# The feed-forward projection scaled in place in its PSUM bank, and the causal convolution reading it from there

## The chip, the cores and the metric

The kernel runs on one core of one Trainium2 chip. The metric is the device time of one execution in microseconds, as the median of several runs. The profile that goes with it records one execution on that core: every instruction of TensorE (PE, with its weight loads as PEld), VectorE (DVE), ScalarE (ACT), GpSimd (POOL) and SyncE (SP, which issues transfers), with its start, its length and the line of the kernel that it comes from.

## The reference

A decoder trunk of two layers over 512 positions of 1024 features, in float32. Layer 0 mixes with a dilated sliding-window attention, layer 1 with a state-space scan; each mixer is followed by a gated feed-forward layer with a short causal convolution, and the trunk ends in an RMS norm. What the change touches is the feed-forward layer:

```python
def rmsnorm(x, w):
    y = x * lax.rsqrt(jnp.mean(x * x, axis=-1, keepdims=True) + NORM_EPS)
    return y * w

def causal_depthwise_conv(x, w, b):        # w: (3, channels) here
    k = w.shape[0]
    y = lax.conv_general_dilated(x, w[:, None, :], window_strides=(1,), padding=[(k - 1, 0)],
        dimension_numbers=("NWC", "WIO", "NWC"), feature_group_count=x.shape[-1])
    return y + b

def conv_ffn(h, w_up, conv_w, conv_b, w_down):
    u = causal_depthwise_conv(h @ w_up, conv_w, conv_b)
    gate, up = u[..., :D_FF], u[..., D_FF:]
    return (jax.nn.silu(gate) * up) @ w_down
```

with h = rmsnorm(x, ffn_norm_w), 2 x 2816 projected channels, and x = x + conv_ffn(h).

## The kernel before

Everything is kept transposed: features on the 128 partitions, the 512 positions along the free axis. The residual x is eight tiles xr (128 x 512). Every large product is made as three matmuls of float32r parts (`mm3`, line 136): the weights and the operand are each split into a high and a low part, and high x high, high x low and low x high are added up in one bank. So one *unit* of a projection, that is 128 output channels for all positions, takes 8 x 3 = 24 matmuls into one bank of 512 float32 columns (`project`, 146).

The norm is applied late. The operand of the projection is x times the norm's weight, split into xh and xl (`split`, 212); the factor 1/rms of each position is worked out while the projection already runs (`inv_rms`, 228), transposed along the free axis on TensorE (`along_free`, 256) and copied to the tile rbc by ScalarE (line 185 for layer 0, line 1046 for layer 1). Each finished unit is then multiplied by rbc.

PSUM has three rings of banks: "mm" with three banks (`mm_bank`, 67), "aux" with three, "side" with two. Units and down projections take turns in the mm ring. At the start of a feed-forward layer the first units cannot be scaled until rbc is there. In layer 0 `norm_and_project` (158) puts unit 0 into an mm bank and units 1 and 2 into side banks; in layer 1 `last_rows` (993) does the same for units 0, 1 and 2 and puts unit 3 into an mm bank, with four of its eight steps ahead of the transposition of the norm's factor and four behind it.

A feed-forward layer (`ffn`, 610) has 44 units, gate and up by turns, in three parts of 16, 16 and 12 units. For each unit:

- `load_unit` (116): SyncE's queue brings 512 KB of weights (line 121), ScalarE casts them to the high part hi (125), VectorE subtracts to get the low part lo (126).
- TensorE: 24 matmuls into the unit's bank p (134).
- VectorE, line 620: us = p x rbc, from the bank into an SBUF tile us, a ring of three tiles.
- `conv` (602) reads us: ScalarE makes the tile a from the last tap's weight and the bias (603), then VectorE adds the two shifted taps, first over 511 columns, then over 510 (605).

For each pair ScalarE applies silu to the gate (624), GpSimd multiplies it with the up half (627), ScalarE and GpSimd split the product into high and low parts (629, 630). After each part, `down` (263) makes the eight output tiles from those parts with two output tiles open at a time, and VectorE adds them to xr (640). The third part of layer 1 goes into the last norm and the output (`finish`, 1059).

The order of the instructions is not written out, except where a manual_schedule block fixes an engine's own order: TensorE's in `norm_and_project`, `last_rows` and the down projections. Elsewhere a scheduler orders each engine's list at build time by a simulated timeline, with the rings of tiles and banks as it goes; what it chose is what the trace shows. Each engine then works through its list in order, and waits for the instruction at its head.

Of the kernel before, what the change touches and what calls it, by code (L numbers as in the profile page):

```python
# [12 lines left out]
ALU = mybir.AluOpType  # L13
# [27 lines left out]
C_FCW = C_SCB + 32  # L41
C_FCB = C_FCW + 2 * 44 * 3
# [9 lines left out]
def trunk(ctx: ExitStack, tc: tile.TileContext, A, out):  # L52
    nc = tc.nc
    V, SC, G, T = nc.vector, nc.scalar, nc.gpsimd, nc.tensor
# [21 lines left out]
    def t2(name, tag, bufs, pool=k2, dtype=F32):  # L76
        return pool.tile([P, 512], dtype, tag=tag, name=name, bufs=bufs)
# [3 lines left out]
    def high_low(name):  # L81

        high = t2(f"{name}h", "high", 8, dtype=F32R)
        if not kept:
            k2.tile([P, 32], F32, tag="gap3", name="gap3", bufs=1)
        kept.append(name)
        return high, t2(f"{name}l", "low", 8, dtype=F32R)
# [13 lines left out]
    rbc = cp.tile([P, S], F32, tag="rbc", name="rbc")  # L101
# [8 lines left out]
    def col(c):  # L110
        return par[:, c : c + 1]
# [4 lines left out]
    def load_unit(src, name, n=1024, pieces=1, low=V, at=0):  # L116
        raw = wr.tile([P, 1024], F32, tag="raw", name=f"raw_{name}")
        hi, lo = (wh.tile([P, 1088], F32R, tag=t, name=f"{t}_{name}")[:, at : at + 1024] for t in ("hi", "lo"))
        for i in range(pieces):
            s = slice(i * n // pieces, (i + 1) * n // pieces)  # L120
            dma(raw[:, s], src[:, s])
            if i < pieces - 1:
                V.tensor_copy(hi[:, s], raw[:, s])
            else:
                SC.copy(hi[:, s], raw[:, s])  # L125
            low.tensor_tensor(lo[:, s], raw[:, s], hi.bitcast(F32)[:, s], op=ALU.subtract)  # L126
        return hi, lo
# [18 lines left out]
    def project(src, name, low=V, cut=None):  # L146

        if name in early:
            return early.pop(name)
        hi, lo = loaded.pop(name) if name in loaded else load_unit(src, name, low=low)  # L150
        t = mm_bank(name)
        for k in range(KD):
            if cut and cut[0] == k:
                cut[1]()
            mm3(t, hi, lo, k, xh[k], xl[k], k == 0, k == KD - 1)
        return t
# [106 lines left out]
    def down(n, load, ms, operand, kn, done, width=512, depth=1, late=False):  # L263

        held = []

        def finish():
            m, p, hi, lo, at = held.pop(0)
            mm3(p, hi, lo, at + kn - 1, *operand(kn - 1), kn == 1, True)
            done(m, p)  # L270

        for m in ms:
            hi, lo, at = load(m)
            p = mm_bank(f"{n}{m}")[:, :width]
            for c in range(kn - 1):
                if late and m == 2 and c == 3:
                    finish()
                    finish()
                mm3(p, hi, lo, at + c, *operand(c), c == 0, False)
            if len(held) == depth and not (late and m == 1):  # L280
                finish()
            held.append((m, p, hi, lo, at))
        while held:
            finish()
# [302 lines left out]
    lp = ctx.enter_context(tc.tile_pool(name="lp", bufs=1, reuse_waits="tile"))  # L587
# [5 lines left out]
    for m in range(KD):  # L593
        if m not in wo_held:
            wo_first(m)
        hi, lo, p = wo_held[m]
# [5 lines left out]
    def conv(dst, src, c_w, c_b, taps):  # L602
        SC.activation(dst, src, AF.Identity, bias=col(c_b), scale=col(c_w + taps - 1))  # L603
        for j in range(1, taps):
            V.scalar_tensor_tensor(  # L605
                dst[:, j:], src[:, : S - j], col(c_w + taps - 1 - j), dst[:, j:],
                op0=ALU.mult, op1=ALU.add,
            )

    def ffn(layer, done):  # L610
        for part, (c0, cn) in enumerate(FF_PARTS):
            gh, gl = [], []
            for c in range(c0, c0 + cn):
                ab = []
                for gu in range(2):
                    i = 2 * c + gu
                    n = f"u{layer}_{i}"
                    p = project(A["wup"][layer * 44 + i], n)
                    us = t2("us" + n, "us", 3, lp)
                    V.tensor_tensor(us, p, rbc, op=ALU.mult)  # L620
                    a = t2("a" + n, "a", 13, lp)
                    conv(a, us, C_FCW + (layer * 44 + i) * 3, C_FCB + layer * 44 + i, 3)
                    ab.append(a)
                SC.activation(ab[0], ab[0], AF.Silu)

                by = V if layer == 1 and c == NFF - 1 else G
                by.tensor_tensor(ab[1], ab[0], ab[1], op=ALU.mult)  # L627
                g_h, g_l = high_low(f"g{c}")
                SC.copy(g_h, ab[1])
                by.tensor_tensor(g_l, ab[1], g_h.bitcast(F32), op=ALU.subtract)  # L630
                gh.append(g_h)
                gl.append(g_l)
            n = cn * P

            def load(m):
                i = (layer * len(FF_PARTS) + part) * KD + m
                return (*load_unit(A["wdn"][i][:, :n], f"wd{i}", n), 0)

            def add(m, p):
                V.tensor_tensor(xr[m], xr[m], p, op=ALU.add)  # L640
                if part == len(FF_PARTS) - 1:
                    done(m)

            if layer == 1 and part == len(FF_PARTS) - 1:
                finish(load, lambda c: (gh[c], gl[c]), cn)
                return
            with tc.manual_schedule(engines={mybir.EngineType.PE}):
                down(f"wd{layer}{part}", load, range(KD), lambda c: (gh[c], gl[c]), cn, add, late=True)
# [4 lines left out]
    norm_and_project(ssum, ups(0, range(3)), ups(0, (3, 4)))  # L653
    ssum_a = t2("ssum2", "ssum", 2)
    ffn(0, lambda m: prep(m, xr[m], C_MIX + KD, ssum_a))
    norm_and_project(ssum_a, [(A["win"][0], "xs00"), (A["wdt"], "wdt"), (A["win"][2], "b0")], [(A["win"][3], "c0"), (A["win"][1], "xs01")])

# [401 lines left out]
    def finish(load, operand, cn):  # L1059
# [72 lines left out]
        for b in range(2):  # L1132
            for j in range(2):
# [6 lines left out]
                queue.dma_start(out[1][j, :, b * 512 : (b + 1) * 512], o)  # L1140

    ffn(1, None)


# [101 lines left out]
```

## Time and profile before

| | |
|---|---|
| median of 3 runs | 1626.72 us (1626.13 to 1626.76) |
| the profiled execution | 1626.55 us |
| its span, first to last instruction | 1624.6 us |
| TensorE busy | 1615.7 us, 99% of the span |
| VectorE busy | 1082.8 us, 67% |
| ScalarE busy | 655.0 us, 40% |
| GpSimd busy | 418.6 us, 26% |
| mean granted TensorE clock | 0.999 |

Busy time of TensorE counts the whole length of a matmul, and matmuls overlap: one lasts 0.38 us by the profile, and the next starts 0.22 us after it. A row of the chain or of a timeline gives the start in us from the span's first instruction, the length in us and what ran; "x3" is three instructions in a row, and what stands in brackets is the idle time of the engine before it with what ended it. The names are those of the kernel's tiles with their numbers left out: u is a unit's bank, usu its us tile, au its a tile, hi_u and lo_u its weights.

### The profile page before, as it was taken

The numbers are of one execution on the slowest core, as the hardware profiler recorded it, in microseconds if no ns is written. First come the engines' busy times: TensorE is split into PE (matmuls) and PEld (weight loads), VectorE is DVE, ScalarE is ACT, GpSimd is POOL, SyncE is SP. The second block draws the span as 40 slices with busy tenths as digits, with TensorE's granted clock in tenths as the row PEclk, the third lists the DMA queues.
The fourth block names the chain that finished last, engine by engine and source line by source line (L and its number), as shares of the span: only waits on it lengthen the run. The fifth ranks groups of instructions, "written<-read, shape, count | busy, mean of one in ns | idle before, by whom it ended". The sixth has DMA issues, their size and how long they took to land.

```text
span 1624.6 us, 21067 instructions
## 1 busy us (share of the span) xinstructions
PE 1615.7 (99%) x8038; PEld 1382.9 (85%) x8038; DVE 1082.8 (67%) x1813; ACT 655.0 (40%) x965; POOL 418.6 (26%) x272
## 2 busy tenths in 40 slices
PE   9999999999999999999999999999999999999998
PEld 8888888888888888888887888888888888888887
DVE  6366665266647855764657899988897784574564
ACT  5233332333334532432445455544443442342343
POOL 0444453045402320220231222222111341121020
PEclk9999999999999999999999999999999999999999
DMA  7322222222224323223233433334332232332321
GB/s 259 98 80 83 78 91 80 96 85 79 78 78 134 113 91 105 103 81 117 81 101 104 148 108 115 100 100 127 114 126 90 93 104 91 104 104 91 104 78 52
DMA packets 53235, 165.13 MB, mean 102 GB/s; under 512 B 6224, under 2 KB 9680, under 8 KB 53136
## 3 DMA queue, kind: packets, MB, share of 16 engines
q1 hardware_dynamic: 52304, 163.01, 30.5%
q8 instruction: 63, 1.03, 0.3%
q10 hardware_dynamic: 832, 0.79, 0.1%
q14 instruction: 36, 0.29, 0.1%
HBM read 161.62 MB, written 2.16 MB: 101 GB/s over the span
## 4 chain that ended last, share of the span: by engine, by line
PE 99%; ACT 0%; DVE 0%; POOL 0%; POOLq 0%; DVEq 0%; issue 0%
PE u L134 29%; PE qk L134 16%; PE wd L134 12%; PE v L134 8%; PE xs L134 5%; PE z L134 5%; PE wso L134 5%; PE wo L134 3%; PE c L134 3%; PE b L134 3%; PE wz L134 2%; PE py L830 1%; PE pg L490 1%; PE pp L477 1%; PE po L485 1%; PE pf L838 1%
## 5 line engine op out<-in xcount | busy, mean ns | idle before, releaser
L134 PE MATMUL u<-xh,lo_u 128*128 128x512 f32 x704 | 268.9, 382 | 0.0
L134 PE MATMUL u<-xh,hi_u 128*128 128x512 f32 x704 | 268.8, 382 | 0.0
L134 PE MATMUL u<-xl,hi_u 128*128 128x512 f32 x704 | 266.3, 378 | 0.0
L627 POOL TENSOR_TENSOR au<-au,au 128x512 f32<-128x512 f32 x43 | 58.5, 1360 | 422.2 <-DVE au L605 396.6
L605 DVE SCALAR_TENSOR_TENSOR au<-usu,par,au 128x511 f32<-128x511 f32 (+1 forms) x176 | 159.4, 911 | 7.6 <-ACT au L603 2.9
L125 ACT CAST hi_u<-raw_u 128x1024 fp32r<-128x1024 f32 x88 | 91.1, 1044 | 168.4 <-PE u L134 95.6
L388 POOL TENSOR_TENSOR rotqk<-rotqk,sr 32x512 f32<-32x512 f32 x48 | 88.2, 1837 | 250.2 <-DVE rotqk L387 239.8
L134 PEld LDWEIGHTS u<-xl,hi_u 128*128 128x128 f32 x704 | 131.7, 187 | 24.5
L134 PEld LDWEIGHTS u<-xh,lo_u 128*128 128x128 f32 x704 | 131.7, 187 | 24.0
L134 PEld LDWEIGHTS u<-xh,hi_u 128*128 128x128 f32 x704 | 131.7, 187 | 21.8 <-issue 0.4
L134 PE MATMUL qk<-xh,hi_qk 128*128 128x512 f32 x384 | 148.6, 387 | 0.0
L134 PE MATMUL qk<-xh,lo_qk 128*128 128x512 f32 x384 | 147.1, 383 | 0.0
L134 PE MATMUL qk<-xl,hi_qk 128*128 128x512 f32 x384 | 145.6, 379 | 0.0
L126 DVE TENSOR_TENSOR lo_u<-raw_u,hi_u 128x1024 fp32r<-128x1024 f32 x88 | 113.8, 1299 | 29.9 <-ACT hi_u L125 29.9
L620 DVE TENSOR_TENSOR usu<-u,rbc 128x512 f32<-128x512 f32 x88 | 60.3, 690 | 93.1 <-PE u L134 86.4
L640 DVE TENSOR_TENSOR xr<-xr,wd 128x512 f32<-128x512 f32 x40 | 27.3, 688 | 116.9 <-PE wd L134 116.9
L125 ACT CAST hi_qk<-raw_qk 128x1024 fp32r<-128x1024 f32 x48 | 50.3, 1047 | 130.3 <-PE qk L134 69.3
L134 PEld LDWEIGHTS qk<-xh,lo_qk 128*128 128x128 f32 x384 | 71.8, 187 | 13.3
L134 PEld LDWEIGHTS qk<-xl,hi_qk 128*128 128x128 f32 x384 | 71.9, 187 | 12.8
L389 POOL TENSOR_TENSOR qk<-qk,rotqk 32x512 f32<-32x512 f32 x48 | 81.5, 1698 | 3.8
L125 ACT CAST hi_wd<-raw_wd 128x1024 fp32r<-128x1024 f32 (+1 forms) x48 | 46.1, 972 | 88.7 <-PE wd L134 55.6
L134 PEld LDWEIGHTS qk<-xh,hi_qk 128*128 128x128 f32 x384 | 71.9, 187 | 11.2
(647 smaller groups left out, 3768.5 us busy)
## 6 DMA issues: line engine op xcount, KB each, us to landing
raw_u<-in_wup SPq DMA_DIRECT2D x88, 512.0 KB, 3.3
raw_qk<-in_wqk SPq DMA_DIRECT2D x48, 512.0 KB, 3.3
raw_wd<-in_wdn SPq DMA_DIRECT2D x32, 512.0 KB, 3.2
raw_xs<-in_win SPq DMA_DIRECT2D x16, 512.0 KB, 3.3
raw_z<-in_win SPq DMA_DIRECT2D x16, 512.0 KB, 3.4
lm<-rows SPq DMA_DIRECT2D x32, 256.0 KB, 5.4
raw_wso<-in_wso SPq DMA_DIRECT2D x16, 512.0 KB, 3.3
raw_v<-in_wv SPq DMA_DIRECT2D x12, 512.0 KB, 3.5
```

Of the source, the lines that this page charges most:

```text
L125: SC.copy(hi[:, s], raw[:, s])
L126: low.tensor_tensor(lo[:, s], raw[:, s], hi.bitcast(F32)[:, s], op=ALU.subtract)
L134: T.matmul(in_turns(dst), w, in_turns(x), start=first, stop=last)
L388: G.tensor_tensor(rot[R, :], rot[R, :], sr[R, :], op=ALU.mult)
L389: G.tensor_tensor(at(t)[R], at(t)[R], of(rot)[R], op=ALU.add)
L477: T.transpose(pp[:, b * P : (b + 1) * P], pr[:, b * P : (b + 1) * P], ident)
L485: T.matmul(po[:, ii], v0[h][:, b * P : (b + 1) * P], pts[i][:, (b - i + 1) * P : (b - i + 2) * P], start=b == max(i - 1, 0), stop=b == i,)
L490: T.matmul(pg[:, ii], vt[g, half][i][:, es], pts[i][:, (g + 1) * P : (g + 2) * P], start=g == 1, stop=g == 2,)
L605: V.scalar_tensor_tensor(dst[:, j:], src[:, : S - j], col(c_w + taps - 1 - j), dst[:, j:], op0=ALU.mult, op1=ALU.add,)
L620: V.tensor_tensor(us, p, rbc, op=ALU.mult)
L627: by.tensor_tensor(ab[1], ab[0], ab[1], op=ALU.mult)
L640: V.tensor_tensor(xr[m], xr[m], p, op=ALU.add)
```

## The change

In the feed-forward layers the product with rbc is written back into the unit's bank, and `conv` is given the bank in place of the us tile. The us ring stays for the state-space layer, which uses it at other lines. Nothing else is edited.

```diff
                     i = 2 * c + gu
                     n = f"u{layer}_{i}"
                     p = project(A["wup"][layer * 44 + i], n)
-                    us = t2("us" + n, "us", 3, lp)
-                    V.tensor_tensor(us, p, rbc, op=ALU.mult)
+                    V.tensor_tensor(p, p, rbc, op=ALU.mult)
                     a = t2("a" + n, "a", 13, lp)
-                    conv(a, us, C_FCW + (layer * 44 + i) * 3, C_FCB + layer * 44 + i, 3)
+                    conv(a, p, C_FCW + (layer * 44 + i) * 3, C_FCB + layer * 44 + i, 3)
                     ab.append(a)
```

Before, the last reader of a unit's bank is line 620. After, the last readers are the activation of line 603 and the two taps of line 605.

## The prediction

> **What bounds the kernel now.** I read the page first, then the chain of work that ended last, then who waited for whom on TensorE. From the page:
>
> ```profile
> span 1624.6 us, 21067 instructions
> PE 1615.7 (99%) x8038; PEld 1382.9 (85%) x8038; DVE 1082.8 (67%) x1813; ACT 655.0 (40%) x965; POOL 418.6 (26%) x272
> ```
>
> The program ends when TensorE has got through its list; 8.9 us of the span are not matmul time. The profiled execution took 1626.55 us, 1.95 more than its span and 0.17 below the median of the three runs, 1626.72. The chain (start, length, what) says how dense the feed-forward layers are:
>
> ```profile
> 513.81 8.45 PE u L134 x38
> ...
> 630.60 84.48 PE u L134 x384
> ...
> 1280.40 8.01 PE u L134 x36
> ...
> 1288.85 61.13 PE u L134 x276
> ```
>
> 384 matmuls in 84.48 us is 0.220 us each, so a unit of 24 (one 128-row slice of the projection, one bank) takes 5.28 us. From 630.60 on nothing interrupts TensorE for 16 units, so nothing can be gained there. The waits on TensorE (in total, times, longest) are four rows, of which the first and the last:
>
> ```profile
> PE warm L327 <- DVE mhalf L107: 1.1, 1, 1.1
> ...
> PE pw L1125 <- DVE ms L252: 0.4, 1, 0.4
> ```
>
> None of them has u in it. The feed-forward projection never visibly waits for its scaling or its convolution; the question is only whether the change makes it wait.
>
> **The change, part by part.** The groups of instructions, by shape (busy us, mean ns, idle before):
>
> ```profile
> L605 DVE SCALAR_TENSOR_TENSOR au<-usu,par,au 128x511 f32<-128x511 f32 x88 | 92.4, 1052 | 4.9 <-ACT au L603 2.9
> L603 ACT ACTIVATE au<-usu,par 128x512 f32<-128x512 f32 x88 | 71.2, 813 | 1.9 <-DVE usu L620 1.4
> L605 DVE SCALAR_TENSOR_TENSOR au<-usu,par,au 128x510 f32<-128x510 f32 x88 | 67.7, 771 | 2.7
> L620 DVE TENSOR_TENSOR usu<-u,rbc 128x512 f32<-128x512 f32 x88 | 60.3, 690 | 93.1 <-PE u L134 86.4 <-ACT rbc L185 6.7
> L225 ACT ACTIVATE sq<-xr 128x512 f32<-128x512 f32 x26 | 16.1, 618 | 6.6 <-DVE xr L1068 6.6
> L849 DVE SCALAR_TENSOR_TENSOR yt<-axs,par,py 128x512 f32<-128x512 f32 x16 | 11.4, 742 | 0.5 <-PE py L830 0.3
> ```
>
> No instruction is added or removed: 88 scalings, 88 activations, 176 taps stay.
>
> *The scaling writes its bank.* No row has VectorE writing a bank. The nearest is L620 itself, 690 ns from a bank into an SBUF tile; I take 690. Below it I allow the 0.58 us of ScalarE's copy from a bank (L1046, below), above it the 1052 ns of the first tap.
>
> *The activation reads the bank.* 813 ns today; ScalarE's 512 columns took 618 ns from SBUF and 0.58 us from a bank, so 0.78 to 0.81, and I take 0.81.
>
> *The taps read the bank.* L849 has one operand in a bank and took 742 ns, no more than the fastest from SBUF; I take 0.74. The mean of 1052 is well above that, so VectorE stands to lose up to 88 x (1052 + 771 - 2 x 742) ns = 29.8 us of busy time. It is worth nothing to the end here, as TensorE waits for none of it; it is cover for the rest. The Trainium skill, "SBUF — State Buffer", section "Who interferes with whom", says a VectorE instruction with at most one SBUF input, outside the two-port modes, does not contend with GpSimd, while one with two does; by it the whole 29.8 us goes, and the sum is as it stands.
>
> *The bank is held longer; this is the cost.* Before, a bank is free again after its scaling. Now it is free after scaling, activation and both taps. The ring has three banks, so a unit's bank is wanted back 2 x 5.28 = 10.56 us after the unit's last matmul. In the run of units the chain needs 0.69 + 0.81 + 2 x 0.74 = 3.0 us of its own and one or two other VectorE instructions between: some 5 us. That is hidden by two units of matmuls, and costs nothing while that cover lasts; the same holds where the down projections take over the ring.
>
> It is not covered where a layer starts. There the units run ahead of the norm: the scale row rbc is not known until four or five units are done, and all chains start at once. Layer 1, VectorE, ScalarE and TensorE:
>
> ```profile
> 1289.31 1.23 DVE L126 TENSOR_TENSOR lo_u<-raw_u,hi_u 128x1024 fp32r<-128x1024 f32 x1 [5.60 <-ACT hi_u L125]
> 1290.45 1.88 DVE L620 TENSOR_TENSOR usu<-u,rbc 128x512 f32<-128x512 f32 x3
> 1292.24 0.74 DVE L605 SCALAR_TENSOR_TENSOR au<-usu,par,au 128x511 f32<-128x511 f32 x1
> 1292.96 1.23 DVE L126 TENSOR_TENSOR lo_u<-raw_u,hi_u 128x1024 fp32r<-128x1024 f32 x1
> 1294.10 2.07 DVE L605 SCALAR_TENSOR_TENSOR au<-usu,par,au 128x510 f32<-128x510 f32 x3
> 1296.09 0.68 DVE L620 TENSOR_TENSOR usu<-u,rbc 128x512 f32<-128x512 f32 x1
> ```
>
> ```profile
> 1289.18 0.58 ACT L1046 COPY rbc<-rb 128x512 f32<-128x512 f32 x1
> 1291.17 0.81 ACT L603 ACTIVATE au<-usu,par 128x512 f32<-128x512 f32 x1 [1.41 <-DVE usu L620]
> 1291.89 1.04 ACT L125 CAST hi_u<-raw_u 128x1024 fp32r<-128x1024 f32 x1
> 1292.83 1.51 ACT L603 ACTIVATE au<-usu,par 128x512 f32<-128x512 f32 x2
> ```
>
> ```profile
> 1291.35 0.39 PE L134 MATMUL u<-xh,hi_u 128*128 128x512 f32 x1
> ...
> 1296.53 0.38 PE L134 MATMUL u<-xh,lo_u 128*128 128x512 f32 x1
> 1296.92 0.46 PE L134 MATMUL u<-xh,hi_u 128*128 128x512 f32 x1
> ```
>
> Units 0, 3 and 4 hold the three banks (1 and 2 lie in side banks). The 36 matmuls between the two small groups of the norm are 12 of unit 3 and all of unit 4; 12 more of unit 3 follow, so 1291.35 is the first matmul of unit 5, which needs bank 0. Its scaling had ended at 1290.45 + 0.68 = 1291.13, just in time. 1296.92 is unit 6, 0.17 us late: unit 3's scaling ended at 1296.77, held up by the ring of three us tiles. That small wait goes with the change; the one in its place is larger.
>
> When does unit 0's second tap end? That hangs on the order the scheduler gives VectorE, and layer 0 shows how it chooses:
>
> ```profile
> 523.35 1.89 DVE L620 TENSOR_TENSOR usu<-u,rbc 128x512 f32<-128x512 f32 x3 [6.71 <-ACT rbc L185]
> 525.15 1.21 DVE L126 TENSOR_TENSOR lo_u<-raw_u,hi_u 128x1024 fp32r<-128x1024 f32 x1
> 526.28 0.74 DVE L605 SCALAR_TENSOR_TENSOR au<-usu,par,au 128x511 f32<-128x511 f32 x1
> 526.95 1.21 DVE L126 TENSOR_TENSOR lo_u<-raw_u,hi_u 128x1024 fp32r<-128x1024 f32 x1
> 528.08 2.72 DVE L605 SCALAR_TENSOR_TENSOR au<-usu,par,au 128x511 f32<-128x511 f32 x4
> ```
>
> ```profile
> 523.21 1.05 ACT L125 CAST hi_u<-raw_u 128x1024 fp32r<-128x1024 f32 x1
> 524.16 0.81 ACT L603 ACTIVATE au<-usu,par 128x512 f32<-128x512 f32 x1
> ...
> 525.81 1.53 ACT L603 ACTIVATE au<-usu,par 128x512 f32<-128x512 f32 x2
> ```
>
> ```profile
> 530.12 0.38 PE L134 MATMUL u<-xh,hi_u 128*128 128x512 f32 x1
> ```
>
> At 525.15 it takes a weight subtraction whose cast ended at 524.26, ahead of unit 0's first tap, ready at 524.97. At 528.08 it takes a first tap (511 columns, unit 1's, ready at about 526.6) ahead of unit 0's second (ready at 527.02). So what has been ready longest goes first, wherever it stands in the code. I carry that over. Steps, start to start: scaling 0.60 (1.79 for three), tap 0.66, weight subtraction 1.14; a freed bank reaches TensorE 0.15 us later (1296.77 to 1296.92).
>
> Layer 1: the us ring no longer limits the scalings, so units 4 (ready before rbc) and 3 (its last matmul is the one before 1291.35, so ready at 1291.5) go ahead of the first tap, ready at 1291.98. 1292.24 + 2 x 0.60 = 1293.44; unit 0's first tap to 1294.10; the weight subtraction, ready at 1292.93, to 1295.24; unit 1's first tap, ready at 1293.64, to 1295.90; unit 0's second ends at 1295.90 + 0.74 = 1296.64. Unit 5 starts at 1296.79 in place of 1291.35, unit 6 at 1296.79 + 5.28 = 1302.07 in place of 1296.92: **+5.15 us**. Unit 3's last tap is seven taps on, 1296.56 + 7 x 0.66 + 0.08 = 1301.3, no further wait. Unit 5's matmul stands at the head of TensorE's list, so all that follows moves with it, and nothing later gives it back: the chain is matmuls to the end.
>
> Layer 0: 525.15 + 1.13 + 0.60 (unit 3's scaling, ready at 524.9, a unit's 5.28 before 530.12) + 0.67 + 1.13 + 2 x 0.66, then 0.74 and 0.15: 530.89, where unit 5 starts at 530.12 today: **+0.8 us**. It is smaller because of the 38 matmuls ahead of the scale row 21 are unit 2's and only 17 unit 3's, so the bank is wanted later.
>
> Sum: 1626.55 + 5.15 + 0.8 = **1632.5 us**. Two lesser things I put at nothing: the us tiles are first used later, so the a tiles move in SBUF, and the state-space layer's matmuls are not fed differently; the transfers on SyncE's queue wait for weight subtractions, which move by no more than TensorE does.
>
> **The rivals.** *The clock falls as well.* TensorE would stand still for 5.3 us. Stretches with TensorE's busy time and the granted clock (after the busy columns):
>
> ```profile
> 865.00:870.00 5.00, 4.28 (x26) 3.43 (x25) 2.53 (x4) 2.72 (x4) 0.62 (x1) 1.00 0.60 197
> 1617.28:1620.69 3.41, 0.98 (x8) 0.75 (x7) 1.78 (x4) 1.27 (x2) 1.13 (x2) 1.00 1.03 342
> 1620.70:1624.60 3.90, 0.00 (x0) 0.00 (x0) 0.00 (x0) 0.00 (x0) 0.00 (x0) 0.50 0.64 236
> ```
>
> 0.7 us of idleness cost no clock; a stretch of 3.41 us with 0.98 busy was followed by half the clock. A stop of 5.3 us has such a stretch in it wherever it is cut. If half pace then lasts one such stretch, 3.41 / 2 = 1.7 us are lost: 1634.2. The Trainium skill, "TensorE: Matmul & The Clock Gate", section "A second HAM failure mode: psum-queue depth-cycling", reports a kernel whose cycling through banks made TensorE idle often enough for the gate to swing; by that rule this case would come out, and the tail's rows agree as far as they go. Against it: it is one stop per layer, not a cycle, and no row has one of this length followed by work.
>
> *The taps go first.* If VectorE runs unit 0's taps as soon as it can, the second ends at 1292.24 + 0.66 + 0.74 = 1293.64, or at 1294.84 with a weight subtraction between, as in the rows; unit 6 starts at 1299.07 to 1300.27, up to 0.5 later if unit 3 is late: +2.2 to +3.9. With layer 0 at 0 to 0.8, 1628.7 to 1631.2, middle 1629.9. For it: the longer chain may weigh with the scheduler once TensorE hangs on it. Against it: layer 0's order.
>
> *Not slower.* The scheduler sees the new wait and does unit 0 first of all: scaling at 1289.76, when rbc is there, then 0.68 + 0.81 + 0.66 + 0.74 + 0.15 = 1292.80, 1.45 late, less the 0.17 that goes: 1627.9, inside 0.2%, with layer 0 at nothing. It decides wherever unit 0's bank comes back before about 1294.7 and layer 0 is hidden. Against it: today a weight subtraction precedes the scaling at 1289.31.
>
> *Faster* could only come from the 0.17 and the few waits elsewhere, which the change does not touch.
>
> **How the numbers follow.** A difference of 0.2%, 3.25 us, is about what a measurement can tell. Forecast as summed: 0.36. With the clock: 0.22. Taps first: 0.24. Not slower: 0.12. Faster 0.03, worse than all (a scaling into a bank at the tap's 1052 ns, five of them ahead, or stops in the run of units) 0.03. Of the taps-first case a third lies under 3.25 us, so same is 0.12 + 0.08 = 0.20, slower 0.77. The range leaves out 0.18: from 1628.6, the bottom of taps first, to 1635.2, the clock's 1634.2 and 1.0 for slower scalings.
>
> **What would show it.** Right: about 5 us between unit 4's or 3's last matmul and unit 5's first, at some 1292 to 1297 of layer 1, with L620 five times in a row before the first tap; a wait of u on VectorE's L605; 0 to 1 us in layer 0; 0.220 us a matmul elsewhere; taps near 742 ns. A clock below 1.00 there decides for that rival. Wrong: no wait on L605 in TensorE's list, or waits all along the run of units.

## The result, and the profile after

The kernel with the change takes 1634.83 us (median of 4 runs, 1633.8 to 1636.88) against 1626.74 for the kernel before beside it (4 runs, 1626.13 to 1626.93): a ratio of 1.0052, with an interval of 1.0035 to 1.0069, so 8.1 us or 0.5% slower. The same kernel, run once more later, gave 1.0048 (1.0036 to 1.0061). The profiled execution took 1633.8 us. Its page:

```profile
span 1632.0 us, 21084 instructions
PE 1617.3 (99%) x8038; PEld 1383.7 (85%) x8038; DVE 1052.1 (64%) x1813; ACT 655.0 (40%) x965; POOL 417.7 (26%) x272
```

VectorE has 30.7 us less to do, the matmuls are as many as before, and the span is 7.4 us longer. Who waited for whom on TensorE (total, times, longest) has one row more than before; the other four are the old ones:

```profile
PE u L134 <- DVE au L605: 5.9, 2, 5.3
...
```

Two waits, then, both on a second tap. TensorE's timeline shows where (start, length, what, and in brackets the idle time before it):

```profile
529.28 0.38 PE L134 MATMUL u<-xh,lo_u 128*128 128x512 f32 x1
530.26 0.46 PE L134 MATMUL u<-xh,hi_u 128*128 128x512 f32 x1 [0.59 <-DVE au L605]
...
1291.22 0.38 PE L134 MATMUL u<-xh,lo_u 128*128 128x512 f32 x1
1296.87 0.77 PE L134 MATMUL u<-xh,hi_u 128*128 128x512 f32 x1 [5.27 <-DVE au L605]
```

Each pair is the last matmul before unit 5 and the first of unit 5. In layer 0 the starts are 0.97 us apart, in layer 1 5.65; at a matmul every 0.22 us that is 0.75 and 5.43 us lost. VectorE's timeline in layer 1, the counterpart of the rows that the order was read from:

```profile
1289.40 1.23 DVE L126 TENSOR_TENSOR lo_u<-raw_u,hi_u 128x1024 fp32r<-128x1024 f32 x1 [5.60 <-ACT hi_u L125]
1290.54 3.08 DVE L619 TENSOR_TENSOR u<-u,rbc 128x512 f32<-128x512 f32 x5
1293.54 0.74 DVE L605 SCALAR_TENSOR_TENSOR au<-u,par,au 128x511 f32<-128x511 f32 x1
1294.19 1.22 DVE L126 TENSOR_TENSOR lo_u<-raw_u,hi_u 128x1024 fp32r<-128x1024 f32 x1
1295.33 6.00 DVE L605 SCALAR_TENSOR_TENSOR au<-u,par,au 128x511 f32<-128x511 f32 x9
```

Five scalings in a row, one tap, a weight subtraction, then taps. The chain of waits leaves TensorE here, runs over exactly these instructions, and comes back with unit 5:

```profile
1290.63 1.49 DVE u L619 x3
1292.12 0.23 issue
1292.34 1.29 DVE u L619 x2
1293.63 0.65 DVE au L605
1294.28 1.13 DVE lo_u L126
1295.41 1.33 DVE au L605 x2
1296.74 0.14 issue
1296.87 60.48 PE u L134 x264
```

The last row holds a second loss. 264 matmuls at 0.22 us are 58.1 us, not 60.48. Cutting the time around the stop into stretches of 3.41 us shows it (start and end; busy us of TensorE and its weight loads, VectorE, ScalarE, GpSimd; then the granted clock, the DMA share and GB/s):

```profile
1291.10:1294.51 3.41, 0.51 (x3) 0.10 (x1) 3.41 (x7) 3.24 (x5) 0.00 (x0) 1.00 0.45 154
1294.51:1297.92 3.41, 1.05 (x3) 0.88 (x4) 3.41 (x5) 1.79 (x3) 0.00 (x0) 0.50 0.43 141
1297.92:1301.33 3.41, 3.41 (x10) 2.64 (x9) 3.41 (x6) 1.15 (x2) 1.78 (x2) 0.50 0.03 13
1301.33:1304.74 3.41, 3.41 (x17) 2.91 (x16) 0.14 (x1) 1.71 (x4) 3.28 (x3) 1.00 0.02 5
```

One stretch nearly without a matmul at full clock, two at half, then full again. Of the two stretches that are filled with matmuls, the one at half clock is touched by 10 of them, the last one by 17. From unit 5's first matmul at 1296.87 to the first one back at 0.22 us, at 1301.54, there are 11 steps in 4.67 us instead of 2.42: 2.25 us lost.

Together: 0.75 + 5.43 + 2.25 - 0.37 = 8.06 us, against 8.1 measured. The 0.37 is what the kernel before lost at this place and the changed one does not: from its first matmul of unit 5, at 1291.35, to its third of unit 6, at 1297.44, it has 26 steps in 6.09 us instead of 5.72. The old wait of 0.17 us at unit 6 is part of it.

A second way to count agrees. From a layer's first projection matmul to the first of its down projection, the traces have 85.56 us before and 86.40 after in layer 0, 89.82 (1260.16 to 1349.98) and 97.11 (1260.25 to 1357.36) in layer 1: +0.84 and +7.29, 8.13 us in all. The rows of the chain for layer 1, two of the kernel before and two of the changed one:

```profile
1260.16 0.66 PE u L134 x3
...
1349.98 15.18 PE wd L134 x69
...
1260.25 0.66 PE u L134 x3
...
1357.36 7.70 PE wd L134 x35
```

This second measure, called the layer's stretch below, is used for the experiments. The spans of the two profiled executions differ by less, 7.4 us. Most of the missing 0.7 us lies ahead of the feed-forward layers, in a part that the change does not touch: this execution of the changed kernel reached the first projection matmul of layer 0 at 502.19 us, the one of the kernel before at 502.80.

The groups by shape answer to the four that were priced (busy us, mean ns, idle before):

```profile
L603 ACT ACTIVATE au<-u,par 128x512 f32<-128x512 f32 x88 | 67.8, 777 | 2.3 <-DVE u L619 1.4
L605 DVE SCALAR_TENSOR_TENSOR au<-u,par,au 128x510 f32<-128x510 f32 x88 | 65.6, 748 | 2.8
L605 DVE SCALAR_TENSOR_TENSOR au<-u,par,au 128x511 f32<-128x511 f32 x88 | 65.4, 746 | 3.9 <-ACT au L603 2.8
L619 DVE TENSOR_TENSOR u<-u,rbc 128x512 f32<-128x512 f32 x88 | 60.9, 698 | 138.8 <-PE u L134 132.1 <-ACT rbc L185 6.7
```

### The profile page after: what moved, and what is told of

Same layout as the page of the kernel before. It is cut to its first block, busy times and chain, and to the rows that moved or that the text cites. A ratio compares the mean times of both kernels' runs of the same rounds, so it can differ in the third digit from the quotient of the medians.

```text
span 1632.0 us, 21084 instructions
## 1 busy us (share of the span) xinstructions
PE 1617.3 (99%) x8038; PEld 1383.7 (85%) x8038; DVE 1052.1 (64%) x1813; ACT 655.0 (40%) x965; POOL 417.7 (26%) x272
## 4 chain that ended last, share of the span: by engine, by line
PE 98%; DVE 1%; ACT 0%; POOL 0%; issue 0%; POOLq 0%; DVEq 0%
PE u L134 28%; PE qk L134 16%; PE wd L134 12%; PE v L134 8%; PE xs L134 5%; PE z L134 5%; PE wso L134 5%; PE wo L134 3%; PE c L134 3%; PE b L134 3%; PE wz L134 2%; PE py L829 1%; PE pg L490 1%; PE pp L477 1%; PE po L485 1%; PE pf L837 1%
## 5 line engine op out<-in xcount | busy, mean ns | idle before, releaser
L619 DVE TENSOR_TENSOR u<-u,rbc 128x512 f32<-128x512 f32 x88 | 60.9, 698 | 138.8 <-PE u L134 132.1
L605 DVE SCALAR_TENSOR_TENSOR au<-u,par,au 128x510 f32<-128x510 f32 (+1 forms) x176 | 130.4, 747 | 6.7 <-ACT au L603 2.8
L126 DVE TENSOR_TENSOR lo_u<-raw_u,hi_u 128x1024 fp32r<-128x1024 f32 x88 | 110.0, 1255 | 27.3 <-ACT hi_u L125 27.3
```

What stands on the lines that cost most here:

```text
L605: V.scalar_tensor_tensor(dst[:, j:], src[:, : S - j], col(c_w + taps - 1 - j), dst[:, j:], op0=ALU.mult, op1=ALU.add,)
L619: V.tensor_tensor(p, p, rbc, op=ALU.mult)
```

## The experiments

**One layer at a time.** Two kernels do the change in one layer only. In the other the us tile stays:

```diff
-                    us = t2("us" + n, "us", 3, lp)
+                    us = p if layer == 0 else t2("us" + n, "us", 3, lp)
```

(`layer == 1` in the second.) Layer 0 alone:

> In place in layer 0 alone; layer 1 keeps its us tiles. If the cost is the stop where a layer starts (0.97 us between two matmuls in layer 0 of the changed kernel, 0.22 in a run, so 0.75 lost): 1627.5 us, with that one stop left and a clock of 1.00 throughout. If the cost comes with every unit that is scaled in place, half of the 8.1 us goes with half of the units: about 1630.8 us.

1627.57 against 1626.31 us, a ratio of 1.0006 (0.9997 to 1.0016). The profiled execution of this run took 5987 us, with the matmuls of a unit at 1.09 to 1.10 us on average, for a reason that its trace does not show. So the kernel was run once more for its trace:

> In place in layer 0 alone, once more for its trace: one stop of 0.97 us at unit 5 of layer 0, no wait of u in layer 1 over 0.3 us, clock 1.00; some 0.8 us over the kernel before.

It took 1627.62 us beside 1626.6, in a single run. TensorE's timeline has the one small stop, layer 0's stretch is 0.93 us longer than in the kernel before, and layer 1's is 89.82 us as there:

```profile
530.02 0.38 PE L134 MATMUL u<-xh,lo_u 128*128 128x512 f32 x1
530.99 0.46 PE L134 MATMUL u<-xh,hi_u 128*128 128x512 f32 x1 [0.59 <-DVE au L605]
```

Layer 1 alone:

> In place in layer 1 alone. Stop at the start of the layer: 5.65 - 0.22 = 5.43 us, plus the slow matmuls behind it (eleven, 2.4 us more than at 0.22 each), less the 0.17 us wait that goes: 1634.4 us, 1632.7 if the clock does not fall in every run. Cost with every unit: about 1630.8 us.

1633.6 against 1626.31, 1.0043 (1.003 to 1.0057): 7.3 us, with a layer 1 stretch of 97.01 (+7.19). By the times, layer 0's part is not clear of noise, as its interval takes in 1. By the stretches the two parts, 0.93 and 7.19, add up to the whole, and layer 1 carries nearly all of it.

**The run of units alone.** In place only from unit 5 of each layer on, which is 78 of the 88 units:

```diff
-                    us = t2("us" + n, "us", 3, lp)
+                    us = p if i >= 5 else t2("us" + n, "us", 3, lp)
```

> Units 0 to 4 of each layer keep their us tiles, all later ones are scaled in place (78 of 88). Stop at the start of the layers: the first banks come back after the scaling as before, so 1626.5 to 1626.9 us, no wait of u on VectorE over 0.3 us, taps from unit 5 on near 742 ns, and VectorE's busy time some 25 us lower than before with nothing gained. Cost with every unit: 78/88 of the 8.1 us, about 1634 us.

1626.37 against 1626.31, 1.0001 (0.9992 to 1.001). TensorE waits four times, as before, and never on a tap. The page shows that most of VectorE's saving is there:

```profile
PE 1616.3 (99%) x8038; PEld 1383.2 (85%) x8038; DVE 1056.3 (65%) x1813; ACT 655.0 (40%) x965; POOL 417.9 (26%) x272
```

So holding the bank longer costs nothing along the run, and 26.5 us less work for VectorE (1082.8 to 1056.3) brings nothing.

**Other banks at the start.** If the cost is that the first units keep their banks too long, taking one of them out of the ring of three must remove it. The auxiliary ring has only the norms' small rows at that time; unit 0 of layer 0 and unit 3 of layer 1 are put there:

```diff
-(side_bank if i else mm_bank)(name)
+(side_bank if i else aux_bank if name[0] == "u" else mm_bank)(name)
...
-side_bank(name) if i in (1, 2) else mm_bank(name)
+side_bank(name) if i in (1, 2) else (aux_bank if i == 3 else mm_bank)(name)
```

> The changed kernel, but with one more bank at each layer's start: unit 0 of layer 0 and unit 3 of layer 1 lie in a bank of the aux ring in place of the mm ring. Unit 5 of each layer then has a free bank. Layer 0: unit 6 wants unit 3's bank at 535.4, free by about 534.3; layer 1: unit 6 wants unit 0's at about 1296.8, free at about 1296.8. So if the cost is the number of banks at the start, both stops go, down to 0.3 us, the clock stays at 1.00, and the time is 1626.5 to 1627.2 us. If the order on VectorE or the in-place writes cost by themselves: over 1630 us.

A miss: 1628.03 against 1626.27, 1.0012 (1.0003 to 1.0021). Both stops are gone, but a new one stands at unit 7 of layer 1, which wants unit 4's bank:

```profile
1301.36 0.38 PE L134 MATMUL u<-xh,lo_u 128*128 128x512 f32 x1
1303.59 0.46 PE L134 MATMUL u<-xh,hi_u 128*128 128x512 f32 x1 [1.85 <-DVE au L605]
```

VectorE's heap of work at the start is not smaller; with TensorE no longer standing still for unit 0, it met the next bank. The 2.23 us between the starts left the clock alone (stretches, columns as above):

```profile
1301.70:1303.59 1.89, 0.04 (x1) 0.03 (x1) 1.89 (x4) 0.95 (x2) 0.66 (x1) 1.00 0.24 50
1303.60:1308.00 4.40, 4.40 (x20) 3.77 (x21) 4.29 (x6) 1.87 (x3) 3.67 (x3) 1.00 0.53 170
```

The next kernel puts unit 4 of layer 1 into that ring too, by one more line in `project`:

```diff
-        t = mm_bank(name)
+        t = (aux_bank if name == "u1_4" else mm_bank)(name)
```

> As the run with one more bank per layer, but in layer 1 unit 4 lies in the aux ring too. There unit 7 still stood 2.0 us for unit 4's bank; now it gets unit 0's, free since about 1296.7, and unit 8 unit 5's, wanted at about 1307 and free at about 1306. If the banks at the start are the whole cost: no wait of u on VectorE over 0.3 us, clock 1.00, within 0.5 us of the kernel before (0.9997 to 1.0003 of it). If in-place units cost anything else, or the backlog only moves on to unit 8: 1 to 2 us over it.

1626.67 against 1626.6, 0.9999 (0.999 to 1.0007). Of the waits one of 0.2 us is left, at unit 8:

```profile
PE u L134 <- DVE au L605: 0.2, 1, 0.2
```

All 88 units are scaled in place here. So the banks of the first units are the whole cost of the change, and with them spared it is, within that interval, neither slower nor faster than before.

**The clock by itself.** To keep TensorE busy in layer 1's stop without touching the wait, 22 matmuls that nobody reads go into an auxiliary bank, written in `last_rows` behind the last matmuls of unit 3:

```diff
         part(3, *range(4, KD))
+        idle = aux_bank("idle")
+        for _ in range(22):
+            long_product(idle, xh[0][:, 0:P], xh[0], True, True)
```

> The changed kernel with 22 matmuls that nobody reads, at TensorE's place behind unit 3 of layer 1, that is in the stop: extra work of 22 x 0.22 = 4.84 us. If the stop is a wait for unit 0's bank and the slow clock comes from the idleness: the fillers vanish in the stop, some 0.6 us of it is left, the clock stays at 1.00, and 2.4 us are won: 1632.7 us. If the clock falls for another reason: 1634.8 us with a slow stretch as before. If TensorE were not really free in the stop: 1634.8 + 4.8 = 1639.6 us.

1633.01 against 1626.31, 1.0042 (1.0026 to 1.0057). By the times alone that cannot be told from the changed kernel. The trace can. The stretches under the fill and after it:

```profile
1291.60:1297.00 5.40, 5.40 (x26) 4.45 (x24) 5.40 (x9) 4.41 (x6) 0.00 (x0) 1.00 0.27 97
1297.70:1301.00 3.30, 3.30 (x15) 2.75 (x16) 3.30 (x6) 0.65 (x2) 0.74 (x1) 1.00 0.35 137
```

The clock stays at 1.00, 15 matmuls are counted in 3.3 us, and layer 1's stretch is 95.02 us, 2.09 less than 97.11. What is left of the loss there, 95.02 - 89.82 = 5.2 us, is the wait alone.

**The order on VectorE.** The prediction rested on scalings of units 3 and 4 going ahead of unit 0's taps. The scheduler can be told to put an instruction behind another; here those two scalings of layer 1 go behind unit 0's last tap (`behind_first` is an ordering edge to it, and nothing for other units):

```diff
+                    with behind_first(layer, (3, 4), i):
-                    V.tensor_tensor(p, p, rbc, op=ALU.mult)
+                        V.tensor_tensor(p, p, rbc, op=ALU.mult)
```

> The changed kernel with only the scalings of units 3 and 4 of layer 1 queued behind unit 0's last tap; the weight subtractions stay free. If those two scalings are what put unit 0's tap late: it ends at about 1294.85 in place of 1296.73, unit 5 starts 1.9 us earlier after a stop of some 3.8 us, and unit 6 waits 0.3 to 1.5 us more for unit 3's bank: 1631 to 1632 us without a fall of the clock, 1633 to 1634 with one. If the backlog only moves on, as in the two runs with a hand-made order: a stop of 5 us or more at unit 6 or 7, and 1635 us or over.

1632.36 against 1626.6, 1.0034 (1.0021 to 1.0048). VectorE's timeline, from unit 0's first tap on:

```profile
1292.50 0.74 DVE L611 SCALAR_TENSOR_TENSOR au<-u,par,au 128x511 f32<-128x511 f32 x1
1293.17 1.23 DVE L126 TENSOR_TENSOR lo_u<-raw_u,hi_u 128x1024 fp32r<-128x1024 f32 x1
1294.31 0.74 DVE L611 SCALAR_TENSOR_TENSOR au<-u,par,au 128x510 f32<-128x510 f32 x1
1294.97 1.29 DVE L627 TENSOR_TENSOR u<-u,rbc 128x512 f32<-128x512 f32 x2
```

Unit 0's second tap ends at 1295.05 instead of about 1296.7, and unit 5 starts at 1295.20. The stop is 3.83 us between starts, and the granted clock differs as well:

```profile
1291.95:1295.36 3.41, 0.16 (x1) 0.19 (x2) 3.41 (x6) 2.75 (x5) 0.00 (x0) 1.00 0.39 142
1295.36:1298.78 3.42, 3.42 (x9) 2.65 (x9) 3.42 (x6) 1.85 (x3) 0.00 (x0) 0.50 0.43 153
1298.78:1302.19 3.41, 3.41 (x17) 2.90 (x16) 2.73 (x5) 1.73 (x3) 2.45 (x2) 1.00 0.02 5
```

One stretch at half clock, not two, and it begins 0.16 us after TensorE is back at work. From 1295.20 to 1298.92 there are 9 steps in 3.72 us instead of 1.98, 1.74 us lost. Layer 1's stretch is 94.79, 2.32 below the changed kernel's: 1.82 of the stop and 0.51 of the clock. The time lies below the 1633 to 1634 us expected with a fall of the clock, as the further wait that was expected at unit 6 did not come.

Two stronger orders were tried before that. In the first, the weight subtractions of units 6 and 7 are put behind unit 0's last tap as well:

```diff
+                    with behind_first(layer, (6, 7), i):
-                    p = project(A["wup"][layer * 44 + i], n)
+                        p = project(A["wup"][layer * 44 + i], n)
```

> The changed kernel with VectorE's order altered in layer 1 alone: the scalings of units 3 and 4 and the weight subtractions of units 6 and 7 queue behind unit 0's last tap. If the length of the stop comes from what ran ahead of that tap: unit 0's last tap ends at about 1293.1 in place of 1296.7, unit 5 starts 3.6 us earlier, and unit 6 waits for unit 3's bank until about 1301.3: two stops of some 2.0 and 2.7 us in place of one of 5.65. The sum is then only 0.8 us shorter, but neither stop is long enough for the clock: 1631.6 us. If the clock falls also after a stop of 2.7 us: about 1633.5. If the order does not matter: 1634.8.

A miss: 1637.09 against 1626.27, 1.0065 (1.0049 to 1.008). Unit 5 now waits only 1.06 us between starts, but unit 6, which wants unit 3's bank, 6.98. On VectorE, the rows after unit 0's taps:

```profile
1293.06 0.69 DVE L628 TENSOR_TENSOR u<-u,rbc 128x512 f32<-128x512 f32 x1
1293.66 3.49 DVE L126 TENSOR_TENSOR lo_u<-raw_u,hi_u 128x1024 fp32r<-128x1024 f32 x3
1297.06 0.70 DVE L628 TENSOR_TENSOR u<-u,rbc 128x512 f32<-128x512 f32 x1
```

By the rule of what has been ready longest, the subtractions that had been put off were then first, and three went ahead of the taps of the next bank. In the second, units 0 and 3 are written first, and the scalings of 1, 2 and 4 and the subtractions of 6 and 7 go behind unit 3's last tap:

```diff
+        if layer == 1:
+            ahead_of.update({i: taps(layer, i) for i in (0, 3)})
...
+        with behind_first(layer, (6, 7), i):
+            p = project(A["wup"][layer * 44 + i], n)
+        with behind_first(layer, (1, 2, 4), i):
+            V.tensor_tensor(p, p, rbc, op=ALU.mult)
```

> As the run before, but units 0 and 3 of layer 1 are both done first (they hold the banks that units 5 and 6 want; units 1 and 2 lie in side banks that nobody wants soon), and the scalings of 1, 2 and 4 and the weight subtractions of 6 and 7 queue behind unit 3's last tap. Unit 5 starts about 2.1 us late, unit 6 does not wait, the clock stays at 1.00: 1626.55 + 0.75 + 2.0 = 1629.3 us. If unit 4's bank or a weight subtraction is late in turn, up to 1.5 us more. If the order does not matter: 1634.8 us.

A miss again: 1636.4 against 1626.27, 1.0061 (1.0047 to 1.0075). Between starts unit 5 waits 0.76 us, unit 6 not at all, and unit 7, on unit 4's bank, 6.25:

```profile
1296.34 1.89 DVE L622 TENSOR_TENSOR u<-u,rbc 128x512 f32<-128x512 f32 x3
1298.13 4.62 DVE L126 TENSOR_TENSOR lo_u<-raw_u,hi_u 128x1024 fp32r<-128x1024 f32 x4
1302.67 1.40 DVE L611 SCALAR_TENSOR_TENSOR au<-u,par,au 128x511 f32<-128x511 f32 x2
```

Both show the same: an early bank 0 is paid for by a late bank 3 or 4. As they move weight subtractions too, they do not price the order of taps and scalings; the kernel with the scalings alone does.

**The changed kernel again**, on the chip of the last comparisons:

> The changed kernel once more, on the same chip as the others: 8.1 us over the kernel before (6.5 to 10), with one stop of about 5.65 us in layer 1 and one of 0.97 in layer 0, and one slow stretch of the clock that ends 6.83 us after it began.

1634.75 against 1626.6, 1.0048 (1.0036 to 1.0061). The stops are 5.65 and 0.97 us between starts again, and layer 1's stretch is 97.42. The last matmul before the long stop starts at 1291.59, unit 5's first at 1297.24, and the half clock lies so (columns as above):

```profile
1291.78:1295.19 3.41, 0.19 (x1) 0.00 (x0) 3.41 (x6) 3.41 (x5) 0.00 (x0) 1.00 0.45 154
1295.19:1298.60 3.41, 1.36 (x3) 1.16 (x4) 3.41 (x6) 1.48 (x3) 0.00 (x0) 0.50 0.50 153
1298.60:1302.02 3.42, 3.42 (x9) 2.64 (x8) 3.09 (x5) 1.47 (x3) 2.10 (x2) 0.50 0.00 1
1302.02:1305.43 3.41, 3.41 (x17) 2.82 (x15) 0.25 (x1) 1.49 (x3) 2.95 (x3) 1.00 0.02 5
```

Again two stretches, 6.83 us. But here the fall comes 3.60 us after the start of that last matmul, and in the first execution (1291.22 to 1294.51) 3.29 us.

## Why the prediction was right, and where it was not

The forecast was 1632.5 us with slower at 0.77; measured were 1634.83, inside the range. The sum's two terms held. What did not hold is the choice between the sum alone and the sum with the clock: the sum gave a loss of 5.95 us where 8.1 were measured. That the range has the result is in part luck, as its top was taken from the rival with the clock, which the sum left out.

- *TensorE bounds the kernel, and the run of units hides the longer hold.* Right, and shown by the kernel that does the change from unit 5 on: 1.0001, no wait on a tap.
- *The prices.* Scaling into its bank 698 ns (690 taken), taps 746 and 748 (742). The taps' busy time fell from 160.1 to 131.0 us, by 29.1 (up to 29.8 forecast), VectorE's in all by 30.7, worth nothing. The activation took 777 ns where I took 0.81 us, which moves nothing.
- *The order in layer 1.* Right instruction by instruction: five scalings, unit 0's first tap, a weight subtraction, unit 1's first tap, unit 0's second. Unit 5 was to start at 1296.79 and started at 1296.87, in a trace that runs 0.09 us behind the one before at this place (the matmul ahead of unit 5 starts at 1291.22 and at 1291.13). The term was +5.15; the trace gives 5.43 - 0.37 = 5.06, and the kernel with the fill 5.2. That this order sets the time is shown by the kernel with two scalings put back, 2.32 us shorter in layer 1.
- *Layer 0.* +0.8 forecast; 0.75 by the stop, 0.84 by the stretch. The kernels with layer 0 alone give 0.93 by the stretch, 1.0 and 1.26 by their times.
- *The clock.* This is the step that failed. The sum gave it nothing, and the rival in which the clock falls as well, at 1634.2, got 0.22 against 0.36. It is what happened. The row that spoke for it was there (a stretch of 3.41 us with 0.98 busy, then 0.50); what I set against it, that there is one stop and no cycle of stops, was no argument, since one is enough. The rival's price was also short: 1.7 us for one stretch, while there were two, of which 2.4 us (1294.51 to 1296.87) fell into the stop itself and 6.83 - 2.36 = 4.47 us on matmuls, at half pace 2.2 us lost.

Of the other rivals, *taps first* did not come, by the order above; when made to come in part it gave 1632.36, above the 1628.7 to 1631.2 that I had priced without the clock; less the 1.74 us of the clock it is 1630.6, inside that price. *Not slower* was priced as if only unit 0's bank counted (and its sum, 1626.55 + 1.45 - 0.17, is 1627.8, not 1627.9): in the two reordered kernels that bank came back almost in time, and the next one was late. A version that is not slower exists, but it needs other banks, not another order that I found.

Why two stretches ran at half clock in one case and one in the other can be followed in the traces. In the changed kernel the granted clock changes at 1294.51, 1301.33 and 1629.01 us, in its second execution at 1295.19, 1302.02 and 1629.70: each time 2 and 96 times 3.413 us apart. In the kernel with two scalings put back it changes at 1295.36, 1298.78 and 1626.46: 1 and 96 times. So the changes lie on a grid of 3.41 us, at another place in each execution. The grid does not start with the stop: the fall came 3.29 us after the start of the last matmul in one execution and 3.60 in another, and with the scalings put back only when TensorE was at work again.

The changed kernel's stop ends in the second stretch of its grid, which has 1.05 us of matmuls and stays at half clock, as does the one after it. The stop of the kernel with two scalings put back ends 0.16 us before the first stretch does; the second is full of matmuls, and the clock is back behind it. The Trainium skill, "TensorE: Matmul & The Clock Gate", section "What's actually happening", has such a free-running window of 3413 ns, after which an idle TensorE is slowed and a busy one released; the traces agree in the 3.41 us. No run here moved a stop of one length so far against that grid that two stretches became one, so that the place of the stop alone decides is argued and not shown.

## What to carry to other kernels

To hold a bank longer costs nothing while the ring's other banks cover the chain, so look for the place where the cover is thinnest: the start of a layer, where several units wait for one scale and all their chains start at once. There, write out the order of the engine that frees the banks, instruction by instruction, and price the bank that is wanted first and then the next two, because relief for one moves the wait to the next. If the sum contains a stop of TensorE as long as those here (3.83 us between starts and more), add the slow matmuls after it to the sum, and do not leave them to a rival.

## What the runs showed of the hardware

A single stop is enough to halve the granted clock, and where the half clock ends was sharp: 3.41 us in one kernel (3.83 us between starts) and 6.83 in another (5.65), 1.74 and 2.25 us lost on the matmuls behind. Stops of 0.97 and 2.23 us between starts cost no clock. Within one execution the clock changed only at whole multiples of 3.41 us from its other changes. A stretch of that grid with 0.16, 0.19 or 0.51 us of matmuls was followed by half the clock; at half clock, stretches with 1.05 and 1.36 us of matmuls did not bring the full clock back, and full ones did. A tap with one operand in a bank took 746 to 748 ns on average over 88, where the same instruction from SBUF had averaged 1052 and 771; and ScalarE's activation was 36 ns shorter from a bank (777) than from SBUF (813).
